# A two-layer hybrid trunk on one core: kept weight chunks of layer two's first query/key pair in slots of their own, two more slots for the token sums, the forget gate's tile in another slot

## The chip, the cores and the metric

The kernel runs on one core of one Trainium2 chip. The metric is device time in microseconds (us) of one execution. Before the change three runs took 1605.53, 1605.92 and 1603.42 us; the median is 1605.53. The trace is one profiled execution of the same program.

Engines are named as the profile names them: PE is TensorE's matmul, PEld its weight load, DVE is VectorE, ACT is ScalarE, POOL is GpSimd and SP is SyncE, which issues most of the DMAs. L246 is line 246 of the kernel.

## The reference

Two layers (DEPTH = 2) over 512 tokens of width 2048, in float32. Each layer normalises x, maps it through one input projection, and splits the result by columns into a gated linear attention group and a chunked attention group, each with a SiLU gate. Their outputs go through one output projection and are added to x:

```python
h = rmsnorm(x, g_pre)
z = h @ w_in
gq, gk, gv, gg, ga, aq, ak, av, ag = split_columns(z)
log_a = jax.nn.log_sigmoid((ga @ w_alpha + b_alpha).astype(jnp.float32)) / GLA_TAU
o_gla = gla_chunk_causal(...)            # chunk-wise state recurrence with the forget gate log_a
o_gla = rmsnorm(o_gla, ...) * jax.nn.silu(gg)
o_att = chunk_band_attention(...)        # softmax over the own chunk and the 8 before, with a relative bias
o_att = rmsnorm(o_att, ...) * jax.nn.silu(ag)
y = jnp.concatenate([o_gla, o_att], axis=-1) @ w_out
return x + rmsnorm(y, g_post)
```

## The kernel before

**Products.** The weights are cut into column blocks of 512 (the blocks of `AG1` and `AG2` have 264) and into chunks of 256 rows. Every float32 operand is split into a high part (a cast on ACT, line 236, written `wh` for weights) and a low part (a subtraction on DVE, line 246, `wl`), and a product takes three matmuls: high by high, low by high, high by low.

Two blocks that lie side by side make a pair. A pair is not multiplied in eight block products of the four quarters of tokens and features, but in seven, P1 to P7, each over four chunks (c = 0 to 3), as in Strassen's method in Winograd's form. On the token side this needs four sums, S1 to S4, per chunk; on the weight side sums are made while the pair runs. One weight chunk is kept through the whole pair: P1 loads it (`H`), P5 adds another chunk to it, P6 adds a third, P7 subtracts it from a fourth, P2 adds to it again, and P4 uses it last. So the four `H` tiles of a pair stay in use from its first product to its last. Other weight chunks (`raw`) and sums (`sa`) live in rings for one or two products.

A job is one product with one chunk. For each of the pair's jobs the stream loads (`load`), adds and casts (`high`), makes the low part (`low`), and then PE runs twelve matmuls (24 of half the width for the query/key pairs, which are computed feature by feature, line 430). Loads, casts and low parts are made three to five jobs ahead of PE (`ahead`).

**Layer two, in the order of the program.** The standard product of block `AG0` (line 353) and the pair `AV0, AV1` are interleaved, since the second half of the tokens comes late out of layer one. Then comes the narrow gate pair `AG1, AG2` (matmuls of 264 columns), then the first query/key pair `QK01, QK23`, then the second, `QK45, QK67`.

**Token sums.** `token_sums(1)` runs as a task beside the second half of `AG0` and the rest of the `AV0` pair. For each chunk c it makes S1, S3, S2 and S4 in this order: a subtraction or addition on DVE, the high part on ACT (line 108), the low part on DVE (line 109). Then POOL issues a DMA that writes the sum to DRAM (line 618), from where later pairs load it again. S1 and S2 also stay in slots of their own (`HOMES`: S1 in g9, g14, g15, g2, S2 in g12, g13, g8, g11) and are read there by P5 and P6 of the `AV0` and the gate pair. S3 and S4 only pass through staging slots, which are used in turn: g10, g16 and a tile of the `H` ring. A staging slot can be written again when its DMA to DRAM has landed.

**Rings and slots.** `H` is a ring of four tiles, `raw` of five, `sa` and `wh` of four, `wl` of three. The gate pair's four kept chunks take the four `H` tiles, and each comes free when the gate pair's P4 has cast it. `slot(tag)` is a fixed place of SBUF that takes a new tile when the last reader of the old one is through. g0 and g1 hold two operands (`A21`, chunks 2 and 3) of the standard product `AG0`, and later values of the attention group.

**What sets the order.** Each engine runs its instructions in the order in which they stand in the program. A scheduler sets that order when the program is built, from a timeline of its own; so a change of a tile's place also moves other instructions. SP issues DMAs in its own order; a DMA that has to wait for a free tile holds up those behind it.

**Forget gate.** `load_forget_gate(l)` (line 758) loads w_alpha into the tile `raw`, in slot g12, which is also the home of S2 of chunk 0; `forget_gate` uses it at the end of the gate pair.

Of the kernel before, what the change touches and what calls it, by code (L numbers as in the profile page):

```python
# [36 lines left out]
def hybrid_trunk(  # L37
# [113 lines left out]
    class Job:  # L151
# [23 lines left out]
        def load(self):  # L175
            k, c, p, b0, b1 = self.kind, self.c, self.pair, self.b0, self.b1
            end = b0 >= NB_IN and k != "std"
            if end:
                c = OC[c]
            top, bottom = (c + 4, c) if end else (c, c + 4)  # L180
            mid = end and b0 == W23[0] and self.l < L - 1
            if k == "std":
                self.raw = self.fetch(rtile("raw", bufs=5), b0, c)
            elif k == "P1":
                h = slot(f"g{4 + c}", [2, 512]) if self.parted else rtile("H")
                p["H", self.c] = self.fetch(h, b0, top)
                last_h[0] = last_load[0]
            elif k == "P5" and self.parted:
                h = p["H", c]
                src = w[self.l, b1 - (b1 > AG1), top].rearrange("p (k n) -> p k n", k=2)  # L190
                nc.gpsimd.dma_start(h, src, accum_op=ALU.add)
            elif k == "P5":
                p["r", self.c] = self.fetch(rtile("raw", bufs=5), b1, top)
            elif k == "P6":
                p["r", self.c] = p["b22", self.c] = self.fetch(rtile("raw", bufs=5), b1, bottom)
            elif k == "P7":
                p["r", self.c] = p.pop(("t", self.c), None) or self.fetch(rtile("raw", bufs=5), b0, top)
            elif k == "P2" or (k == "P4" and (end or self.parted)):
                p["r", self.c] = self.fetch(rtile("raw", bufs=5), b0, bottom)
            sums = (so_d if end else sa_d)[self.l]  # L200
            src = sums.get((LEFT.get(k), c))
            if self.l == L - 1:
                home = k in ("P5", "P6") and b0 in (AV0, AG1)
            else:
                home = k == "P5" and b0 == AV0
            if b0 == AG1 and k == "P5":
                p["a22", c] = slot(f"g{4 + c}", [2, 512], F32R)
                nc.sync.dma_start(flat(p["a22", c]), sums["A22", c])
            if b0 == AG1 and k == "P4":
                self.a = p["a22", c]  # L210
            elif src is not None and b0 != NB_IN and not home:
                until(lambda: k == "P4" or (id(sums), LEFT[k], c) in written)
                self.a = rtile("sa", (2, 512), F32R)
                with tc.issue_after(last_h[0]) if mid else nullcontext():
                    last_load[0] = nc.sync.dma_start(flat(self.a), src).ins
            if b0 == W23[0] and k == ("P6" if mid else "P5"):
                with tc.issue_after(last_h[0]):
                    p["t", self.c] = self.fetch(slot(f"a11{self.c}" if mid else SPARE[self.c], [2, 512]), b0, c + 4)
# [36 lines left out]
    for l in range(L):  # L255
        if l:
            pr = {}
            stream += [Job(l, "std", c, AG0) for c in CO]
            stream += [Job(l, k, c, *PAIRS[0], pr) for k, c in PROD_FRONT]
            stream += [Job(l, "std", c, AG0) for c in CO]  # L260
            stream += [Job(l, k, c, *PAIRS[0], pr) for k, c in PROD_REST]
            pr = {}
            stream += [Job(l, k, c, *GATE_PAIR, pr) for k, c in PROD_GATE]
        else:
            stream += [Job(l, "std", c, b) for b in (AG0, AG1, AG2) for c in CO]
        for b0, b1 in PAIRS[1:] if l else PAIRS:
            pr = {}
            stream += [Job(l, k, c, b0, b1, pr) for k, c in PROD]
        for b0, b1 in (W01, W23):
            pr = {}  # L270
            stream += [Job(l, k, c, b0, b1, pr) for k, c in (PROD_OUT if b0 == NB_IN else PROD_END)]
# [363 lines left out]
            yield  # L635

    def token_sums(l):
        tags, home = (("g10", "g16", "H"), HOMES) if l else (STAGE, HOME)
        return make_sums(sa_d[l], tags, lambda c: (full[0, c][:, 0, :], full[0, c][:, 1, :], full[1, c][:, 0, :], full[1, c][:, 1, :]), home)

    VT = ("g16", "g17", "g4", "g5", "g6", "g7", "g12", "g13")
# [114 lines left out]
    fg_weights = {}  # L756

    def load_forget_gate(l):
        raw = slot("g12", [2, 512])
        fac = slot("g13", [2, 512], F32R)  # L760
        nc.sync.dma_start(raw[0:98, 0, :], w_alpha[l])
        nc.gpsimd.memset(raw[96:98, 1, :], 1.0)
        wal, gaT = fac[0:98, 0, :], fac[0:98, 1, :]
        yield
        nc.scalar.copy(wal, raw[0:98, 0, :])
        nc.vector.tensor_tensor(
            out=wal[64:97, :], in0=raw[64:97, 0, :], in1=wal[64:97, :].bitcast(F32), op=ALU.subtract
        )
        fg_weights[l] = (raw, fac, wal, gaT)
        yield  # L770
# [815 lines left out]
```

## Time and profile before

| | |
|---|---|
| median of three runs | 1605.53 us (1603.42 to 1605.92) |
| the profiled execution | 1608.99 us, its span 1607.2 us |
| DMA in the span | 441.38 MB, mean 275 GB/s |
| mean granted clock of PE | 0.998 |
| gate pair (window 924.35 to 971.84) | 47.5 us, P1 to P4 of 264 columns |
| first query/key pair | from 971.84 us |

How to read the views: a row of the timeline gives the start in us from the span's start, the duration of the group, engine, line, operation, tiles written and read, shapes and count, and in brackets how long the engine stood idle before it and what ended that. A window row gives length, then busy time and count of PE, PEld, DVE, ACT and POOL, then the granted clock of PE, the mean busy share of the DMA engines, and GB/s.

### The profile page before, as it was taken

The numbers are of one execution on the slowest core, as the hardware profiler recorded it, in microseconds if no ns is written. First come the engines' busy times: TensorE is split into PE (matmuls) and PEld (weight loads), VectorE is DVE, ScalarE is ACT, GpSimd is POOL, SyncE is SP. The second block draws the span as 40 slices with busy tenths as digits, with TensorE's granted clock in tenths as the row PEclk, the third lists the DMA queues.
The fourth block names the chain that finished last, engine by engine and source line by source line (L and its number), as shares of the span: only waits on it lengthen the run. The fifth ranks groups of instructions, "written<-read, shape, count | busy, mean of one in ns | idle before, by whom it ended". The sixth has DMA issues, their size and how long they took to land.

```text
span 1607.2 us, 25131 instructions
## 1 busy us (share of the span) xinstructions
PE 1592.8 (99%) x9158; PEld 1376.8 (86%) x9158; DVE 1278.0 (80%) x1697; ACT 920.5 (57%) x1535; POOL 134.2 (8%) x206
## 2 busy tenths in 40 slices
PE   9999999999999999999999999999999999999998
PEld 7988999998888777888887899999988887788886
DVE  5978768678677877998988877775876878689887
ACT  7554445657454556664786455456575545465654
POOL 0220000000000001100122000000000100101001
PEclk9999999999999999999999999999999999999999
DMA  9798686685868769689889987857858686686887
GB/s 351 232 407 304 220 295 216 228 307 170 275 220 281 270 210 319 217 309 389 306 259 364 361 282 280 308 186 260 301 202 298 202 305 242 227 299 241 331 303 205
DMA packets 137228, 441.38 MB, mean 275 GB/s; under 512 B 14885, under 2 KB 27429, under 8 KB 137073
## 3 DMA queue, kind: packets, MB, share of 16 engines
q1 hardware_dynamic: 119952, 377.86, 67.0%
q0 software_dynamic: 16864, 61.63, 10.9%
q8 instruction: 72, 1.18, 0.3%
q14 instruction: 52, 0.42, 0.1%
q10 hardware_dynamic: 288, 0.30, 0.1%
HBM read 380.20 MB, written 61.62 MB: 275 GB/s over the span
## 4 chain that ended last, share of the span: by engine, by line
PE 88%; issue 4%; DMA 3%; DVE 3%; ACT 1%; POOL 1%; POOLq 0%; SPq 0%; ACTq 0%; DVEq 0%
PE mm L440 51%; PE mm L430 20%; PE mm L353 5%; PE ax L440 3%; PE ax L1007 2%; DMA H<-in_w_dram 2%; PE ax L1193 1%; PE ax L990 1%; PE ax L1165 1%; DVE wl L246 1%; PE ax L970 1%; PE ax L969 1%; PE ax L968 1%; DMA S<-g 1%; ACT wh L236 0%
## 5 line engine op out<-in xcount | busy, mean ns | idle before, releaser
L440 PE MATMUL mm<-wh,sa 128*128 128x512 f32 (+1 forms) x1600 | 510.1, 390 | 1.2 <-DMA sa<-S 0.6
L236 ACT CAST wh<-H 128x1024 fp32r<-128x1024 f32 (+1 forms) x256 | 261.5, 1025 | 207.8 <-PE mm L440 80.3
L246 DVE TENSOR_TENSOR wl<-H,wh 128x1024 fp32r<-128x1024 f32 (+1 forms) x256 | 303.4, 1188 | 92.8 <-PE mm L440 28.1
L440 PEld LDWEIGHTS mm<-wh,sa 128*128 128x128 f32 x1600 | 297.6, 188 | 70.6 <-issue 8.1
L236 ACT CAST wh<-raw 128x1024 fp32r<-128x1024 f32 (+2 forms) x237 | 236.3, 1001 | 194.1 <-PE mm L440 71.7
L246 DVE TENSOR_TENSOR wl<-raw,wh 128x1024 fp32r<-128x1024 f32 (+2 forms) x237 | 272.9, 1154 | 59.2 <-PE mm L440 24.6
L440 PE MATMUL mm<-wl,sa 128*128 128x512 f32 (+1 forms) x800 | 309.2, 387 | 0.0
L430 PE MATMUL mm<-sa,wh 128*128 128x256 f32 x1280 | 238.1, 285 | 0.2 <-ACT wh L236 0.2
L440 PE MATMUL mm<-wh,a 128*128 128x512 f32 (+1 forms) x672 | 218.2, 389 | 0.0
L430 PEld LDWEIGHTS mm<-sa,wh 128*128 128x128 f32 x1280 | 200.6, 192 | 0.9 <-ACT wh L236 0.4
L430 PE MATMUL mm<-sa,wl 128*128 128x256 f32 x640 | 180.8, 283 | 0.0
L440 PEld LDWEIGHTS mm<-wl,sa 128*128 128x128 f32 x800 | 150.3, 188 | 28.8 <-DVE wl L246 0.4
L230 DVE TENSOR_TENSOR H<-H,raw 128x1024 f32<-128x1024 f32 (+1 forms) x144 | 170.2, 1187 | 1.9 <-DMA raw<-in_w_dram 1.2
L440 PEld LDWEIGHTS mm<-wh,a 128*128 128x128 f32 x672 | 124.8, 188 | 25.1
L440 PE MATMUL mm<-wl,a 128*128 128x512 f32 (+1 forms) x336 | 130.2, 388 | 0.0
L430 PEld LDWEIGHTS mm<-sa,wl 128*128 128x128 f32 x640 | 122.2, 191 | 0.2 <-DVE wl L246 0.2
L440 PE MATMUL mm<-wh,g 128*128 128x512 f32 (+1 forms) x416 | 120.3, 367 | 0.2
L484 POOL TENSOR_TENSOR sm<-sm,mhalf 128x2 f32<-128x2 f32 (+2 forms) x40 | 50.1, 1252 | 684.3 <-DVE sm L1017 376.7
L232 DVE TENSOR_TENSOR raw<-H,raw 128x1024 f32<-128x1024 f32 (+1 forms) x56 | 66.4, 1186 | 42.1 <-DMA raw<-in_w_dram 39.8
L390 ACT COPY ev<-mm 128x512 f32<-128x512 f32 (+1 forms) x112 | 64.1, 572 | 59.2 <-PE mm L440 44.1
L430 PE MATMUL mm<-a,wh 128*128 128x256 f32 x512 | 95.7, 287 | 1.4 <-ACT wh L236 1.4
L252 DVE TENSOR_TENSOR H<-H,raw 128x1024 f32<-128x1024 f32 (+1 forms) x48 | 56.6, 1180 | 43.0 <-DMA raw<-in_w_dram 40.7
(273 smaller groups left out, 2411.9 us busy)
## 6 DMA issues: line engine op xcount, KB each, us to landing
raw<-in_w_dram SPq DMA_DIRECT2D x287, 512.0 KB, 5.1
sa<-S SPq DMA_DIRECT2D x188, 512.0 KB, 4.4
H<-in_w_dram SPq DMA_DIRECT2D x60, 512.0 KB, 5.1
sa<-A SPq DMA_DIRECT2D x48, 512.0 KB, 5.6
sa<-oS SPq DMA_DIRECT2D x32, 512.0 KB, 5.4
S<-g POOLq DMA_DIRECT2D x30, 512.0 KB, 7.9
raw<-in_w_ag_dram SPq DMA_DIRECT2D x32, 264.0 KB, 4.2
oS<-g POOLq DMA_DIRECT2D x16, 512.0 KB, 4.7
```

Of the source, the lines that this page charges most:

```text
L230: nc.vector.tensor_tensor(out=h, in0=h, in1=r, op=ALU.add)
L232: nc.vector.tensor_tensor(out=r, in0=h, in1=r, op=ALU.subtract)
L236: last_cast[0] = nc.scalar.copy(self.wh[:, z, :], src[:, z, :]).ins
L246: last_low[0] = nc.vector.tensor_tensor(out=self.wl[:, z, :], in0=self.src[:, z, :], in1=self.wh[:, z, :].bitcast(F32), op=ALU.subtract).ins
L252: nc.vector.tensor_tensor(out=h, in0=h, in1=self.src, op=ALU.add)
L353: nc.tensor.matmul(pss[o], a(part, kk, o) if callable(a) else a[:, part, t], rhs[:, kk, :], start=(i == 0 and kk == 0 and m == 0), stop=(i ...
L390: last_copy[0] = nc.scalar.copy(e, src[t]).ins
L430: nc.tensor.matmul(dst, lhs[:, kk, f], a[:, part, tok], start=(fresh and kk == 0 and m == 0 and ft % 2 == 0), stop=(c == 3 and kk == 1 and ...
L440: last_mm[0] = nc.tensor.matmul(out_ps[t], a[:, part, tok], rhs[:, kk, :], start=(fresh and kk == 0 and m == 0), stop=(c == 3 and kk == 1 ...
L484: nc.gpsimd.tensor_tensor(out=out_r, in0=v, in1=mhalf[:, : v.shape[-1]], op=ALU.pow)
L968: nc.tensor.matmul(ps[:, :n], self.qh[:, t], self.kh[:, :n], start=True, stop=False)
L1007: nc.tensor.matmul(o, self.pt[i][:, j * P : (j + 1) * P], av[hd // 4, j // 2][:, j % 2, (hd % 4) * P : (hd % 4 + 1) * P], start=(j == 0), ...
```

## The change

Three things change, all in layer two.

First, P1 of the first query/key pair loads nothing any more: its four kept chunks are loaded by P3 of the gate pair, into the slots g14, g15, g2 and g12, the homes of S1 of chunks 1 to 3 and of S2 of chunk 0. The dictionary `qk` hands them from one pair to the other. The gate pair's `H` tiles, which used to go to these chunks, go to the kept chunks of the second query/key pair. Second, the staging slots of the token sums are five: g10, g16, `H`, g0, g1. Third, the forget gate's tile is in g10 in layer two.

```diff
             if k == "std":
                 self.raw = self.fetch(rtile("raw", bufs=5), b0, c)
+            elif k == "P1" and ("H", self.c) in p:
+                pass
             elif k == "P1":
                 h = slot(f"g{4 + c}", [2, 512]) if self.parted else rtile("H")
                 p["H", self.c] = self.fetch(h, b0, top)
...
+            if b0 == AG1 and k == "P3":
+                p["next"]["H", c] = self.fetch(slot(("g14", "g15", "g2", "g12")[c], [2, 512]), PAIRS[1][0], c)
...
-            pr = {}
+            qk = {}
+            pr = {"next": qk}
             stream += [Job(l, k, c, *GATE_PAIR, pr) for k, c in PROD_GATE]
...
         for b0, b1 in PAIRS[1:] if l else PAIRS:
-            pr = {}
+            pr = qk if l and b0 == QK01 else {}
             stream += [Job(l, k, c, b0, b1, pr) for k, c in PROD]
...
-        tags, home = (("g10", "g16", "H"), HOMES) if l else (STAGE, HOME)
+        tags, home = (("g10", "g16", "H", "g0", "g1"), HOMES) if l else (STAGE, HOME)
...
-        raw = slot("g12", [2, 512])
+        raw = slot("g10" if l else "g12", [2, 512])
```

The order of the instructions moves with it, from the token sums of layer two to the end of the first query/key pair; outside that stretch it is the same. The lines of the changed kernel stand a few numbers later (246 becomes 250). A name such as g16_1717_8817 is a tile in slot g16 and its serial number.

**ACT and DVE during the token sums** (between the last standard products and the rest of the `AV0` pair). L108 is the high part of a sum, wh the cast of a weight chunk: wh_1720 for P5 of chunk 1, wh_1723 for chunk 2, wh_1729 for chunk 3, wh_1736 for P6 of chunk 0. The serial number after the slot tells the sum: 1713 is S4 of chunk 1, 1716 and 1717 are S1 and S3 of chunk 2, 1725 is S3 of chunk 3. ACT before:

```order
L108 CAST g10_1713_8790<-H_1573_8105 128x512
L108 CAST g16_1717_8817<-g2_1645_8451 128x512
L236 CAST wh_1720_8840<-g5_1668_8546 128x1024
L108 CAST g15_1716_8812<-g2_1645_8451 128x512
L236 CAST wh_1723_8862<-g6_1671_8564 128x1024
L782 ACTIVATE t2_1726_8881<-mm_1693_8681 128x512
L236 CAST wh_1729_8897<-g7_1674_8582 128x1024
```

ACT now:

```order
L108 CAST g0_1713_8790<-H_1573_8105 128x512
L240 CAST wh_1720_8840<-g5_1668_8546 128x1024
L108 CAST g15_1716_8812<-g2_1645_8451 128x512
L108 CAST g1_1717_8817<-g2_1645_8451 128x512
L240 CAST wh_1723_8862<-g6_1671_8564 128x1024
L108 CAST g16_1725_8871<-g3_1653_8485 128x512
L787 ACTIVATE t2_1726_8881<-mm_1693_8681 128x512
L240 CAST wh_1729_8897<-g7_1674_8582 128x1024
```

S3 of chunk 2 stands two places later on ACT, behind P5's cast and S1 of chunk 2, and S3 of chunk 3 has come up. On DVE, which makes the low parts of the same sums (L109) and weights (L250) and the additions to the kept chunks (L234 for P5 and P6, L236 for P7), the twelve rows from S4 of chunk 1 on are now:

```order
L109 TENSOR_TENSOR g0_1713_8790<-H_1573_8105,g0_1713_8790 128x512
L234 TENSOR_TENSOR g4_1660_8521<-g4_1660_8521,raw_1730_8899 128x1024
L109 TENSOR_TENSOR g15_1716_8812<-g2_1645_8451,g15_1716_8812 128x512
L250 TENSOR_TENSOR wl_1722_8860<-g5_1668_8546,wh_1720_8840 128x1024
L109 TENSOR_TENSOR g1_1717_8817<-g2_1645_8451,g1_1717_8817 128x512
L635 TENSOR_TENSOR g2_1645_8451<-g2_1645_8451,H_1581_8144 128x512
L109 TENSOR_TENSOR g16_1725_8871<-g3_1653_8485,g16_1725_8871 128x512
L234 TENSOR_TENSOR g5_1668_8546<-g5_1668_8546,raw_1737_8928 128x1024
L250 TENSOR_TENSOR wl_1728_8895<-g6_1671_8564,wh_1723_8862 128x1024
L236 TENSOR_TENSOR raw_1754_9025<-g4_1660_8521,raw_1754_9025 128x1024
L638 TENSOR_TENSOR H_1581_8144<-H_1581_8144,g2_1645_8451 128x512
L109 TENSOR_TENSOR g8_1718_8828<-g2_1645_8451,g8_1718_8828 128x512
```

Three rows of 1024 columns follow up to the low part for P6 of chunk 0: the low part for P5 of chunk 3, an addition, and that low part itself. Before, the second of these rows was the low part of S3 of chunk 2 (in g16), ahead of the addition to g4.

**SP and PE in the gate pair.** SP issues the raw chunks of AG1 and AG2 (raw, from in_w_ag) and the sums (sa, from S3). SP before, from P3's last raw chunk on:

```order
L164 DMA raw_1853_9525<-in_w_ag_dram 128x528
L164 DMA raw_1859_9562<-in_w_ag_dram 128x528
L164 DMA raw_1863_9583<-in_w_ag_dram 128x528
L761 DMA g12_1934_9963<-in_w_alpha_dram 98x512
L164 DMA raw_1867_9604<-in_w_ag_dram 128x528
L215 DMA sa_1860_9564<-S310_110 128x1024
L164 DMA raw_1871_9625<-in_w_ag_dram 128x528
```

SP now:

```order
L164 DMA raw_1856_9531<-in_w_ag_dram 128x528
L172 DMA g14_1834_9425<-in_w_dram 128x1024
L164 DMA raw_1863_9570<-in_w_ag_dram 128x528
L172 DMA g15_1841_9464<-in_w_dram 128x1024
L164 DMA raw_1867_9591<-in_w_ag_dram 128x528
L172 DMA g2_1852_9511<-in_w_dram 128x1024
L172 DMA g12_1859_9550<-in_w_dram 128x1024
L164 DMA raw_1871_9612<-in_w_ag_dram 128x528
L219 DMA sa_1864_9572<-S310_110 128x1024
L164 DMA raw_1875_9633<-in_w_ag_dram 128x528
```

The four kept chunks have come in between the raw chunks, and w_alpha has gone from there; it is issued some 34 places earlier. At the head of the gate pair PE had, ahead of P4 of chunk 2 of the `AV0` pair (mm_1664, mm_1665, twelve matmuls of which the first two are shown), two matmuls of the gate's first job (mm_1816, mm_1817):

```order
L440 MATMUL mm_1816_9328<-wh_1800_9259,a110_1563_8075 128x264
L440 MATMUL mm_1817_9329<-wh_1800_9259,a110_1563_8075 128x264
L440 MATMUL mm_1664_8528<-wh_1789_9210,sa_1787_9193 128x512
L440 MATMUL mm_1664_8528<-wl_1795_9235,sa_1787_9193 128x512
L440 MATMUL mm_1664_8528<-wh_1789_9210,sa_1787_9193 128x512
```

and now has all twelve of them there (the first six shown):

```order
L445 MATMUL mm_1816_9328<-wh_1800_9259,a110_1563_8075 128x264
L445 MATMUL mm_1817_9329<-wh_1800_9259,a110_1563_8075 128x264
L445 MATMUL mm_1816_9328<-wl_1803_9277,a110_1563_8075 128x264
L445 MATMUL mm_1816_9328<-wh_1800_9259,a110_1563_8075 128x264
L445 MATMUL mm_1817_9329<-wl_1803_9277,a110_1563_8075 128x264
L445 MATMUL mm_1817_9329<-wh_1800_9259,a110_1563_8075 128x264
```

The matmuls that read the low part wl_1803 have moved up, ahead of P4 of chunk 2.

**SP at the start of the first query/key pair.** The raw chunks are those of P5 (the first two) and P6, sa is S1, and the H tiles are kept chunks. Before:

```order
L172 DMA raw_1912_9862<-in_w_dram 128x1024
L172 DMA raw_1921_9909<-in_w_dram 128x1024
L215 DMA sa_1939_9999<-S112_104 128x1024
L172 DMA H_1906_9826<-in_w_dram 128x1024
L215 DMA sa_1944_10041<-S113_105 128x1024
L172 DMA raw_1938_9997<-in_w_dram 128x1024
L172 DMA H_1909_9844<-in_w_dram 128x1024
L172 DMA raw_1943_10039<-in_w_dram 128x1024
L172 DMA H_1916_9883<-in_w_dram 128x1024
```

Now:

```order
L172 DMA raw_1914_9866<-in_w_dram 128x1024
L219 DMA sa_1923_9913<-S111_103 128x1024
L172 DMA raw_1922_9911<-in_w_dram 128x1024
L219 DMA sa_1939_9999<-S112_104 128x1024
L172 DMA H_2043_10768<-in_w_dram 128x1024
L172 DMA raw_1938_9997<-in_w_dram 128x1024
L219 DMA sa_1944_10041<-S113_105 128x1024
L172 DMA H_2051_10813<-in_w_dram 128x1024
L172 DMA raw_1943_10039<-in_w_dram 128x1024
L172 DMA H_2072_10914<-in_w_dram 128x1024
```

The H tiles in these places were the first query/key pair's kept chunks; now they are the second's (their serial numbers are higher), which used to be issued about 40 places later.

On ACT the casts of the first two kept chunks now stand ahead of the gate pair's last evictions and of the table load; before, only the first did. On POOL the memset of the forget gate's tile stands before the last two sums' writes; before, it stood behind them.

## The prediction

> **What bounds the kernel now.** I read the page first: busy times, then the chain that ended last.
>
> ```profile
> PE 1592.8 (99%) x9158; PEld 1376.8 (86%) x9158; DVE 1278.0 (80%) x1697; ACT 920.5 (57%) x1535; POOL 134.2 (8%) x206
> PE 88%; issue 4%; DMA 3%; DVE 3%; ACT 1%; POOL 1%; POOLq 0%; SPq 0%; ACTq 0%; DVEq 0%
> ```
>
> TensorE (PE) is the bound, and the change adds and removes no matmul. So it can only win back time in which PE waits, or runs below its pace. A pipelined PE looks busy even then; pauses have to be read from matmul starts against an undisturbed pace. These windows give the pace: 50 us hold 419 matmuls of the query/key form, two of them still running from before, so 0.12 us each; 21.56 us hold 95 new ones with 512 columns, so 0.227 us each.
>
> ```profile
> 990.00:1040.00 50.00, 50.00 (x419) 50.00 (x419) 35.80 (x35) 25.00 (x29) 0.00 (x0) 1.00 0.80 276
> 852.06:873.62 21.56, 21.56 (x96) 17.83 (x95) 17.46 (x23) 12.52 (x17) 4.36 (x9) 1.00 1.01 386
> ```
>
> **Place 1, the start of the first query/key pair.** PE's timeline, the count of that line's matmuls (L430), and the granted clock (after the busy times) around the pause:
>
> ```profile
> 971.84 0.63 PE L430 MATMUL mm<-a,wh 128*128 128x256 f32 x4
> 976.48 0.74 PE L430 MATMUL mm<-a,wh 128*128 128x256 f32 x4 [1.40 <-ACT wh L236]
> 977.43 1.17 PE L430 MATMUL mm<-sa,wh 128*128 128x256 f32 x4 [0.21 <-ACT wh L236]
> 981.19 0.40 PE L430 MATMUL mm<-a,wh 128*128 128x256 f32 x2
> 971.84:981.30 9.46, 7.85 (x47) 7.29 (x48) 0.82 1.00 392
> 974.80:980.74 5.94, 4.33 (x22) 3.92 (x21) 4.28 (x4) 4.76 (x7) 0.94 (x2) 0.73 0.98 395
> ```
>
> From the first of the 47 starts (971.84) to the last (981.19) are 46 steps: 46 x 0.12 = 5.52 us at pace, 9.35 us in fact. **3.83 us are lost.** The clock row splits them: (1 - 0.73) x 5.94 = 1.6 us at a lowered clock, about 2.2 us of pauses. What ended last before them, from the chain and from ACT's timeline:
>
> ```profile
> 961.06 8.90 DMA H<-in_w_dram
> 957.51 1.63 SPq L172 DMA_DIRECT2D raw<-in_w_dram  x2
> 970.06 1.05 ACT L236 CAST wh<-H 128x1024 fp32r<-128x1024 f32 x1 [1.74 <-DMA H<-in_w_dram]
> 974.09 1.28 ACT L62 ACT_TABLE_LOAD   x1
> 975.38 1.99 ACT L236 CAST wh<-H 128x1024 fp32r<-128x1024 f32 x2
> ```
>
> The SP row is P5's first two raw loads. The pair's first kept chunk is issued at 961.06, lands at 970, and only then can ACT cast it. ACT is in order: behind that late cast came the gate evictions and a table load, so the second chunk was cast at 975.38.
>
> **Place 2, the token sums.**
>
> ```profile
> 881.78 0.61 PE L440 MATMUL mm<-wh,g 128*128 128x512 f32 x2
> 883.47 0.73 PE L440 MATMUL ax<-wh,g 128*128 128x512 f32 x2 [1.07 <-ACT g L108]
> 887.63 0.84 PE L440 MATMUL ax<-wh,g 128*128 128x512 f32 x3
> 882.20:887.50 5.30, 4.12 (x17) 2.94 (x17) 5.30 (x7) 2.29 (x4) 2.14 (x4) 1.00 0.94 303
> 871.89 0.62 ACT L108 CAST g<-g 128x512 fp32r<-128x512 f32 x1 [3.66 <-DMA S<-g]
> 872.54 0.69 DVE L109 TENSOR_TENSOR g<-g,g 128x512 fp32r<-128x512 f32 x1 [2.56 <-ACT g L108]
> 880.80 0.62 ACT L108 CAST H<-H 128x512 fp32r<-128x512 f32 x1 [2.48 <-DVE H L633]
> 882.80 0.61 ACT L108 CAST g<-g 128x512 fp32r<-128x512 f32 x1
> ```
>
> Between 881.78 and 887.63 start 18 matmuls (the window's 17 and the one before them): 18 x 0.227 = 4.08 us at pace, 5.85 in fact, **1.77 us lost**, at full clock. PE waits for S1 of chunk 3, cast at 882.80. That is late because S3 of chunk 2 waited till 871.89 for slot g16, which was still being written out; DVE stood for 2.56 us behind it and was busy without a break afterwards.
>
> **The change, part by part.** *Kept chunks.* The four loads of 512 KB now have slots g14, g15, g2, g12, free once P5 of chunks 1, 2, 3 and P6 of chunk 0 are through in the gate pair. SP issues them between the gate's raw loads, near 936 to 944 us. DMA's share there (the figure before GB/s):
>
> ```profile
> 936.00:940.00 4.00, 4.00 (x35) 4.00 (x35) 3.73 (x6) 1.92 (x4) 0.00 (x0) 1.00 0.42 129
> 940.00:944.00 4.00, 4.00 (x35) 4.00 (x34) 3.45 (x6) 3.10 (x7) 0.52 (x1) 1.00 0.29 73
> 944.00:948.00 4.00, 4.00 (x35) 4.00 (x34) 2.23 (x4) 2.02 (x4) 0.00 (x0) 1.00 0.79 244
> ```
>
> At the 392 GB/s of the saturated window above, 2.1 MB take 5.3 us. Free are 4 x (0.58 + 0.71 + 0.21) = 6.0 us. They fit, just, and land some 25 us before use. The vacated places on SP, from 961 us on, do not stay empty: the next pair's H loads move up into the ring, so P5's raw chunks land as late as before. They have time: P1 of chunks 0 and 1 needs no load and keeps PE busy for 48 x 0.12 = 5.8 us, until 977.6; P5's first raw loads are issued from 957.51 on. ACT now casts both P1 chunks ahead of the evictions and the table load. I take the whole 3.83 us as gone; the other end is 0. Late next would be P5 of chunk 1, wanted four chunks on, at 971.84 + 4 x 2.88 = 983.4. ACT comes to its cast after the table load, which ended at 975.4, and some five casts of 1.05, near 981; DVE's low part takes 1.2 more: about 1 us of room, an estimate.
>
> One rule speaks against part of this. By the Trainium skill's page "TensorE: Matmul & The Clock Gate" (section "HAM oscillation — how this bites in real kernels") only PE pauses over about 3.4 us bring the lower clock back. Here it does not agree with the trace, where pauses of 1.4 and 0.2 us stand beside the 0.73 above. By the rule, the 1.6 us would have another cause and stay, and the sum below would be 3.45.
>
> *Two more slots.* S4 of chunk 1 goes to g0, S3 of chunk 2 to g1. A wait is exchanged, not removed: g1 holds an operand of the standard product until PE has read it, and ACT's queue is behind it.
>
> ```profile
> 870.68 0.39 PE L353 MATMUL mm<-wh,g 128*128 128x512 f32 x1
> 869.30 0.69 DVE L109 TENSOR_TENSOR g<-H,g 128x512 fp32r<-128x512 f32 x1
> 874.29 0.69 DVE L109 TENSOR_TENSOR g<-g,g 128x512 fp32r<-128x512 f32 x1
> 874.89 1.22 DVE L246 TENSOR_TENSOR wl<-g,wh 128x1024 fp32r<-128x1024 f32 x1
> 876.02 0.68 DVE L630 TENSOR_TENSOR g<-g,H 128x512 f32<-128x512 f32 x1
> ```
>
> That read ends at 871.07, only 0.8 us before 871.89. But in the new order a cast of P5's weights and S1 of chunk 2 stand ahead of the waiting one, so DVE has work meanwhile. From 869.9 it has eight operations of 1024 columns (1.14 us apart) and six of 512 (0.60 apart) up to the low part for P6 of chunk 0: 9.1 + 3.6 = 12.7, done at 882.6. PE asks for it at 881.78 + 6 x 0.227 = 883.1. ACT has S1 of chunk 3 by about 880 to 881.6, before the 882.24 at which PE wants it. So I take 1.77 us; the lower end is 0, since the room on DVE is 0.5 us.
>
> *Head of the gate pair.* Here the new order of PE costs. The low part of the gate's first chunk is ready late:
>
> ```profile
> 924.35 0.40 PE L440 MATMUL mm<-wh,a 128*128 128x264 f32 x2
> 924.38 0.71 DVE L246 TENSOR_TENSOR wl<-H,wh 128x528 fp32r<-128x528 f32 x1
> ```
>
> Before, twelve matmuls of P4 stood between the first two and those that need it; now these follow directly, at 924.59, while it ends at 925.09. About 0.55 us lost (everything shifts alike, since DVE's work there follows PE's evictions); ends 0 and 0.7.
>
> *Gate pair's end.* A small stall there hangs on a raw chunk for a DVE addition:
>
> ```profile
> 961.67 0.28 PE L440 MATMUL mm<-wh,g 128*128 128x264 f32 x1
> 962.33 0.39 PE L440 MATMUL ax<-wl,a 128*128 128x264 f32 x1 [0.37 <-DVE wl L246]
> 959.70 0.71 DVE L252 TENSOR_TENSOR H<-H,raw 128x528 f32<-128x528 f32 x1 [1.37 <-DMA raw<-in_w_ag_dram]
> ```
>
> 0.66 - 0.12 = 0.54 us. The raw loads move up a place on SP, the transfers before them grow. I take no change, between -0.54 and +0.5.
>
> *Forget gate tile.* w_alpha goes to g10, far earlier on SP; the wait for g12 (P6 of chunk 0) passes to the last kept chunk. POOL's memset now waits for S4 of chunk 2 to be written out, with the last two sums' writes behind it. Cost nothing: they are read long after.
>
> ```profile
> 895.05 0.53 POOL L618 DMA_DIRECT2D S<-g  x1 [0.21 <-issue]
> ```
>
> **The sum.** 3.83 + 1.77 - 0.55 = 5.05 us. The profiled execution took 1608.99 us (span 1607.2): 1603.9. Against the median of the runs, 1605.53, which is 3.46 shorter: **1600.5 us**.
>
> **Rivals.** *(a) The token sums stay late*: g1's wait or DVE's 0.5 us of room is misjudged. For it speaks the thin room, against it DVE's idle 2.56 us. Then 3.83 - 0.55 = 3.28: 1602.3. *(b) The lowered clock is not caused by these pauses* and returns anyway; the stall at 882, which kept clock 1.00 with a similar pause, speaks for it. 1.6 us stay: 1602.1. That rule of the Trainium skill would have it so. *(c) The change misses its aim*: the pair's start is held by something else (P5's raw chunks, ACT's order). Gain 1.77 - 0.55: 1604.3. *(d) Slower: the 2.1 MB do not fit* into 936 to 948 us. S3's operands and the last raw chunks of the gate pair queue behind them, and DMA is full from 964 on, so the 5.3 us are not made up: PE loses them before the query/key pair, with one lowered clock of 1.6: -5.05 + 5.3 + 1.6 = +1.85, 1607.4. It decides when more than about 3.7 us of transfers are left over: S3's first operand was issued at 944.97 and lands in 4.4, at 949.4; P7's first matmul, the second of the PE row, reads it at 953.1.
>
> ```profile
> 944.97 0.33 SPq L215 DMA_DIRECT2D sa<-S  x1
> sa<-S SPq DMA_DIRECT2D x188, 512.0 KB, 4.4
> 953.02 0.41 PE L440 MATMUL mm<-wh,sa 128*128 128x264 f32 x2
> ```
>
> **How the numbers follow.** Forecast 0.58, (a) 0.17, (b) 0.08, (c) 0.12, (d) 0.05. The low end: all three stalls gone and no loss at the head is 6.14 us, 1599.4, and 1 us for the spread of the runs (1603.42 to 1605.92): 1598.4. The high end takes in (c): 1604.6; (d) is left out. A measurement of this kernel tells 0.2%, 3.2 us, from no change. So faster means under 1602.3: the forecast, half of (a), most of (b), 0.71. Slower, over 1608.7, is the tail of (d), 0.04. The same: 0.25.
>
> **What would show it.** Right: in the changed profile the first query/key matmuls start 0.12 us apart over two chunks at clock 1.00; the kept chunks' issues stand at 934 to 943 us; no PE wait near 882; one of about 0.5 near 923 to 925. Wrong: a wait of PE on a low part at P6 of chunk 0 (a); a clock under 1.00 with no pause (b); ACT waiting for a DMA of raw at the pair's start (c); DVE or PE waiting for raw or sa between 945 and 965 (d).

## The result, and the profile after

Eighteen runs of each kernel: before 1606.76 us median (1603.42 to 1610.6), after 1603.04 us (1601.56 to 1607.24). The ratio is 0.9979, 95% interval 0.9971 to 0.9987: 3.4 us faster, between 2.1 and 4.7. A second measurement of the same change (below, e4) gave 0.9976 (0.9966 to 0.9986), 3.9 us. The prediction had 5.05 us and 1600.5, its range 1598.4 to 1604.6. So the time lies in the range, but the forecast gain lies above the first interval and inside the second (2.2 to 5.5).

The profiled execution after took 1601.56 us, its span 1599.5. That is 7.4 us less than the profiled execution before, twice what the medians say. How that comes about takes up most of what follows.

The head of the page and of the chain that ended last, after:

```profile
PE 1589.6 (99%) x9158; PEld 1375.0 (86%) x9158; DVE 1279.6 (80%) x1697; ACT 921.1 (58%) x1535; POOL 135.5 (8%) x206
PE 93%; DVE 3%; DMA 1%; ACT 1%; issue 1%; SPq 0%; POOLq 0%; DVEq 0%; ACTq 0%
```

PE has the same 9158 matmuls and is still the bound. Windows after, first one over the first 46 steps of the query/key pair, then the three over the stretch where the early loads were expected, then the token sums' stretch (columns as in the table's note above):

```profile
969.01:974.53 5.52, 5.52 (x49) 5.52 (x48) 5.52 (x9) 4.41 (x8) 0.69 (x3) 1.00 1.03 409
936.00:940.00 4.00, 4.00 (x35) 4.00 (x35) 2.97 (x5) 3.18 (x8) 0.00 (x0) 1.00 0.80 230
940.00:944.00 4.00, 4.00 (x35) 4.00 (x34) 2.52 (x5) 1.42 (x4) 0.00 (x0) 1.00 0.88 263
944.00:948.00 4.00, 4.00 (x35) 4.00 (x35) 3.91 (x7) 2.84 (x5) 0.00 (x0) 1.00 1.01 353
868.00:890.00 22.00, 22.00 (x98) 18.21 (x97) 21.64 (x25) 14.31 (x20) 5.77 (x12) 1.00 1.02 391
```

46 steps of 0.12 us are 5.52 us: the window holds those starts and three matmuls more (still running from before, or at its edge), at clock 1.00. Before, the same steps took 9.35. The DMA share between 936 and 948 rose from 0.42, 0.29 and 0.79; the differences sum to 4 x (0.38 + 0.59 + 0.22) = 4.8 us of the 5.3 that the new loads were priced at. PE is busy through all 22 us of the token sums, where it had been busy for 20.82 before:

```profile
868.00:890.00 22.00, 20.82 (x91) 16.61 (x90) 19.44 (x23) 12.22 (x18) 5.36 (x10) 1.00 1.00 378
```

PE's timeline after, the start of the query/key pair and the head of the gate pair; then ACT's row for S3 of chunk 2, now in slot g1, and SP's rows for the early loads:

```profile
969.01 0.64 PE L435 MATMUL mm<-a,wh 128*128 128x256 f32 x4
922.61 0.39 PE L445 MATMUL mm<-wl,a 128*128 128x264 f32 x1 [0.47 <-DVE wl L250]
```

```profile
870.25 0.62 ACT L108 CAST g<-g 128x512 fp32r<-128x512 f32 x1 [1.14 <-PE mm L358]
```

```profile
933.96 0.33 SPq L172 DMA_DIRECT2D g<-in_w_dram  x1
937.10 0.33 SPq L172 DMA_DIRECT2D g<-in_w_dram  x1
939.75 1.90 SPq L172 DMA_DIRECT2D g<-in_w_dram  x2
```

All four places are as forecast: the pair's start at pace, the new stall at the gate pair's head (matmul start to start 0.76 us, 0.64 over pace), the wait for g1 put on PE's read instead of a write-out, the loads between 934 and 942 us.

### The profile page after: what moved, and what is told of

It is laid out like the page before. It is cut to its first block, busy times and chain, and to the rows that moved or that the text cites. A ratio compares the mean times of both kernels' runs of the same rounds, so it can differ in the third digit from the quotient of the medians.

```text
span 1599.5 us, 25116 instructions
## 1 busy us (share of the span) xinstructions
PE 1589.6 (99%) x9158; PEld 1375.0 (86%) x9158; DVE 1279.6 (80%) x1697; ACT 921.1 (58%) x1535; POOL 135.5 (8%) x206
## 3 DMA queue, kind: packets, MB, share of 16 engines
q8 instruction: 72, 1.18, 0.3%
## 4 chain that ended last, share of the span: by engine, by line
PE 93%; DVE 3%; DMA 1%; ACT 1%; issue 1%; SPq 0%; POOLq 0%; DVEq 0%; ACTq 0%
PE mm L445 54%; PE mm L435 19%; PE mm L358 6%; PE ax L445 4%; PE ax L1012 2%; PE ax L1198 1%; DVE wl L250 1%; PE ax L995 1%; PE ax L1170 1%; DMA raw<-in_w_dram 1%; PE ax L975 1%; PE ax L974 1%; PE ax L973 1%; PE ax L1037 0%; PE ax L1290 0%
## 5 line engine op out<-in xcount | busy, mean ns | idle before, releaser
L240 ACT CAST wh<-H 128x1024 fp32r<-128x1024 f32 (+1 forms) x240 | 244.9, 1023 | 194.7 <-PE mm L445 81.2
L250 DVE TENSOR_TENSOR wl<-H,wh 128x1024 fp32r<-128x1024 f32 (+1 forms) x240 | 284.4, 1187 | 86.8 <-PE mm L445 31.3
L250 DVE TENSOR_TENSOR wl<-raw,wh 128x1024 fp32r<-128x1024 f32 (+2 forms) x237 | 273.2, 1156 | 60.2 <-PE mm L445 29.2
L234 DVE TENSOR_TENSOR H<-H,raw 128x1024 f32<-128x1024 f32 (+1 forms) x136 | 161.0, 1188 | 1.4 <-DMA raw<-in_w_dram 0.7
L236 DVE TENSOR_TENSOR raw<-H,raw 128x1024 f32<-128x1024 f32 (+1 forms) x52 | 61.6, 1184 | 34.8 <-DMA raw<-in_w_dram 34.6
L445 PEld LDWEIGHTS mm<-wh,g 128*128 128x128 f32 x416 | 75.3, 188 | 13.4 <-ACT ev L395 0.6
```

Source lines behind the costliest of these rows:

```text
L234: nc.vector.tensor_tensor(out=h, in0=h, in1=r, op=ALU.add)
L236: nc.vector.tensor_tensor(out=r, in0=h, in1=r, op=ALU.subtract)
L240: last_cast[0] = nc.scalar.copy(self.wh[:, z, :], src[:, z, :]).ins
L250: last_low[0] = nc.vector.tensor_tensor(out=self.wl[:, z, :], in0=self.src[:, z, :], in1=self.wh[:, z, :].bitcast(F32), op=ALU.subtract).ins
L445: last_mm[0] = nc.tensor.matmul(out_ps[t], a[:, part, tok], rhs[:, kk, :], start=(fresh and kk == 0 and m == 0), stop=(c == 3 and kk == 1 ...
```

## The experiments

The losses below are worked out from the starts of all matmuls between the 4,801st (844.16 us before, 843.31 after) and the 6,001st (1034.47 and 1028.20; outside this stretch the order did not change): the time from start to start less the number of steps at pace (0.227 us for 512 columns, 0.12 for 256 and 264, 0.06 for 128). Undisturbed steps of 264 columns take 0.121 us on the mean, so some 0.3 us of each profile's gate pair is this rounding; it cancels in differences.

| run | edit | median us (runs) | ratio, 95% interval |
|---|---|---|---|
| e1 | kernel before again | 1606.11 (12) | 0.9993 (0.9982 to 1.0004) |
| e2 | token sums' two slots alone | 1607.75 (12) | 0.9999 (0.9989 to 1.0009) |
| e3 | kept chunks' early loads alone | 1604.91 (12) | 0.9984 (0.9972 to 0.9996) |
| e4 | the change again | 1603.35 (12) | 0.9976 (0.9966 to 0.9986) |
| e5 | first kept chunk loaded twice | 1621.48 (1) | |
| e6 | one token slot less | 1610.26 (1) | |
| e7 | one early chunk | 1605.11 (11) | 0.9983 (0.9973 to 0.9992) |
| e8 | the five slots in another order | 1605.95 (11) | 0.9995 (0.9986 to 1.0004) |
| e9 | one early chunk, five slots | 1604.64 (12) | 0.9980 (0.9969 to 0.9991) |
| e10 to e12 | kernel before, three profiles | 1609.39, 1607.16, 1607.85 | |

The kernel before ran beside them with medians of 1606.97 to 1607.45 us.

### e1, e10, e11, e12: the kernel before, four more profiles

No edit. The question is whether the stalls of the one profile from which the prediction was sized are those of every execution.

> The kernel before, unchanged, for a second profile of it. Open is why the profiled executions lie 7.4 us apart and the medians only 3.7. Theory A (every execution of the kernel before has the three stalls at the sizes of its first profile): again 1.8 us lost at 882, 0.5 at 961.7, and 3.8 at 972 to 981 with a granted clock near 0.73 there; time within 0.1% of before. Theory B (the lowered clock at 975 is not in every execution): the two pauses of 1.4 and 0.2 us stand there again, but the clock is 1.00 in that window and only about 2.2 us are lost; the ratio is 1.000 all the same.

> A third profile of the kernel before. Theory B (what the first profile shows at 882 and at 975 was a draw from a spread): between 0.3 and 1.8 us lost at 868 to 890, 1.5 to 2.6 us of pauses and casts late at 972 to 982, and a lowered clock only if the pauses fall together in one stretch of some 3.4 us, as in the first profile. Theory A: 1.8 and 3.8 as in the first.

> A fourth profile of the kernel before, with the same expectations as the third: theory B gives losses between those of the first two profiles, theory A the first profile's.

> A fifth profile of the kernel before, with the same expectations as the third. Over the five, theory B has the mean of what the change removes between 844 and 1034 us near the 3.4 to 3.9 us of the ratios; theory A has it at 5 or more.

ACT's wait for g16's write-out, in e1, e10, e11 and e12 in turn (before: 3.66):

```profile
870.68 0.62 ACT L108 CAST g<-g 128x512 fp32r<-128x512 f32 x1 [2.28 <-DMA S<-g]
```

```profile
872.48 0.62 ACT L108 CAST g<-g 128x512 fp32r<-128x512 f32 x1 [3.25 <-DMA S<-g]
```

```profile
871.07 0.62 ACT L108 CAST g<-g 128x512 fp32r<-128x512 f32 x1 [2.54 <-DMA S<-g]
```

```profile
872.16 0.62 ACT L108 CAST g<-g 128x512 fp32r<-128x512 f32 x1 [2.19 <-DMA S<-g]
```

PE's losses behind it were 0.38, 1.37, 0.64 and 0.31 us, and 1.77 in the first profile: in each of the five the wait less 1.9 us. So the wait was read rightly, and 1.9 us of it are covered by what DVE and PE have in hand; but the landing of the write-out differs by 1.5 us between executions, and the first profile held the longest of the five.

PE's pause before the second chunk of the query/key pair, in e1, e10, e11 and e12 in turn (before: 1.40; a pause of 0.21 follows in all):

```profile
975.16 0.74 PE L430 MATMUL mm<-a,wh 128*128 128x256 f32 x4 [0.83 <-ACT wh L236]
```

```profile
977.73 0.74 PE L430 MATMUL mm<-a,wh 128*128 128x256 f32 x4 [1.41 <-ACT wh L236]
```

```profile
976.12 0.74 PE L430 MATMUL mm<-a,wh 128*128 128x256 f32 x4 [1.39 <-ACT wh L236]
```

```profile
977.10 0.74 PE L430 MATMUL mm<-a,wh 128*128 128x256 f32 x4 [1.42 <-ACT wh L236]
```

The pause is there in all five. The clock behind it isn't. Windows of 3.4 us over pause and what follows, in the kernel before, e10 and e12:

```profile
974.10:977.50 3.40, 1.79 (x14) 1.38 (x12) 1.12 (x2) 3.27 (x3) 1.61 (x3) 1.00 1.03 414
977.50:980.90 3.40, 3.40 (x16) 3.40 (x17) 3.40 (x4) 2.36 (x4) 0.00 (x0) 0.50 0.92 371
```

```profile
976.34:979.74 3.40, 1.80 (x13) 1.60 (x14) 2.03 (x2) 3.30 (x5) 0.66 (x2) 1.00 1.02 406
979.74:983.14 3.40, 3.40 (x19) 3.40 (x18) 3.40 (x4) 2.12 (x4) 0.00 (x0) 0.50 0.75 261
```

```profile
974.10:977.50 3.40, 1.98 (x17) 1.78 (x16) 1.12 (x2) 3.36 (x6) 2.17 (x4) 1.00 1.02 410
975.70:979.10 3.40, 1.78 (x12) 1.58 (x13) 2.02 (x2) 2.82 (x4) 0.66 (x2) 1.00 1.02 408
977.50:980.90 3.40, 3.19 (x27) 2.98 (x26) 3.40 (x4) 2.82 (x5) 0.00 (x0) 1.00 0.87 346
```

Two of the five (the first and e10) ran at half clock for 3.4 us; e11 and e12, with the same pause, and e1 did not. At half clock the matmuls of this form start 0.213 us apart (16 in 3.4 us) instead of 0.12, so the drop costs 16 x 0.093 = 1.5 us where it comes, where the prediction took 1.6. All losses together:

| losses, us | before | e1 | e10 | e11 | e12 | mean | after | e4 | gain, means | forecast |
|---|---|---|---|---|---|---|---|---|---|---|
| token sums | 1.77 | 0.38 | 1.37 | 0.64 | 0.31 | 0.89 | 0.00 | 0.00 | 0.89 | 1.77 |
| to the gate pair's head | 0.13 | 0.83 | 0.16 | 0.25 | 0.05 | 0.28 | 0.80 | 0.82 | -0.53 | -0.55 |
| rest of the gate pair | 1.37 | 1.34 | 1.18 | 1.46 | 0.76 | 1.22 | 0.47 | 0.48 | 0.75 | 0 |
| query/key start, 100 steps | 3.83 | 1.55 | 4.60 | 2.57 | 3.34 | 3.18 | 0.00 | 0.00 | 3.18 | 3.83 |
| from there on | 0.00 | 0.00 | 0.52 | 0.00 | 0.61 | 0.23 | 0.40 | 0.31 | -0.13 | 0 |
| sum | 7.10 | 4.10 | 7.83 | 4.92 | 5.07 | 5.80 | 1.67 | 1.61 | 4.16 | 5.05 |

Theory B: the five span 4.1 to 7.8 us of losses, and what the change removes on their mean, 4.2 us, lies within both intervals of the timed runs. Its bounds were too narrow, though: e10 lost more than the first profile, and e12 3.34 us at the start without a drop of the clock. Theory A, that each execution has the first profile's sizes, does not hold. The rest of the 7.4 us between the two profiled executions lies outside the stretch that was changed, 0.85 us of it already before 844.

### e4: the change again

> The changed kernel, unchanged, for a second profile beside these. Theory A: no loss over 0.3 us between 860 and 1015 us but the one at the head of the gate pair (0.6), ratio 0.9968. Theory B: the same profile, ratio 0.9979, the sum of the two single parts within 1 us.

Its losses stand in the table: within 0.06 us of the first profile after in sum. In these two profiles, what the change leaves did not vary; in the five before, what it removed did.

### e2 and e3: one part alone

e2 is the kernel before with the slots only:

```diff
-        tags, home = (("g10", "g16", "H"), HOMES) if l else (STAGE, HOME)
+        tags, home = (("g10", "g16", "H", "g0", "g1"), HOMES) if l else (STAGE, HOME)
```

> Only the two more slots for the token sums. Theory A: the stall at 882 goes (-1.8 us), the one at the head of the gate pair comes (+0.6), the start of the query/key pair stays as it was: -1.2 us, ratio 0.9993. Rival (the token sums are late for another reason than slot g16's write-out): a stall of 1 us or more stays near 882 and the kernel is not faster, ratio 1.000 or 1.0004 with the head's stall.

e3 is the change with that line as before.

> Only the kept chunks' loads in slots g14, g15, g2, g12, with the forget gate's tile in g10; the token sums keep three slots. Theory A: 1.8 us at 882 stay, no stall at the head of the gate pair, the 3.8 us at the query/key pair's start and perhaps the 0.5 us at 961.7 go: -3.8 to -4.4 us, ratio 0.9975. Theory B (lowered clock only in some executions): -2.2 to -2.8 us, ratio 0.9984. Rival (P5's raw chunks hold the start): under 1 us, ratio above 0.9994.

e3 removes the start's whole loss, and is 0.9984, 2.6 us faster (0.6 to 4.5); theory B's number. e2 has no loss at the token sums, 0.81 at the gate pair's head as expected, and still gains nothing. PE's timeline, then SP's, in e2:

```profile
954.49 0.39 PE L440 MATMUL mm<-wl,sa 128*128 128x264 f32 x1 [0.35 <-DVE wl L246]
959.83 0.51 PE L440 MATMUL mm<-wh,sa 128*128 128x264 f32 x2 [1.10 <-DMA sa<-S]
```

```profile
951.65 3.13 SPq L164 DMA_DIRECT2D raw<-in_w_ag_dram  x2
954.88 0.38 SPq L215 DMA_DIRECT2D sa<-S  x1
```

With the token sums' slots the scheduler also puts a raw load of the gate pair ahead of the last operand's load (`sa`) on SP. The raw load waits for a free tile, the operand behind it is issued at 954.88, and PE waits for it until 959.83. The rest of the gate pair loses 2.46 us, where the five profiles of the kernel before have 1.22. What PE loses there it waits less at the query/key pair's start (0.69 us), since it comes there later, at 972.97. That the start's loss shrinks when PE is late, because the kept chunk's landing does not move with PE, is argued from this and not shown by itself. Over the whole stretch e2's profile even loses less than the mean of the five, 4.35 us against 5.80, while the timed runs have a difference of 0.2 us, between 1.8 faster and 1.4 slower. So the late operand by itself does not explain why no gain is seen, and that stays open.

So the gains don't simply add up: -0.2 and -2.6 us of the parts against -3.4 and -3.9 of the whole, though the intervals leave room for a sum.

### e5: the first kept chunk one load later

```diff
             elif k == "P1":
                 h = slot(f"g{4 + c}", [2, 512]) if self.parted else rtile("H")
+                if self.l and b0 == QK01 and c == 0:
+                    self.fetch(h, b0, top)
                 p["H", self.c] = self.fetch(h, b0, top)
```

> The kernel before, with the query/key pair's first kept chunk loaded twice into its tile, so that it is complete one load (4 to 9 us) later. Theory (the landing of the kept chunk holds the pair's start): PE loses 4 to 8 us more around 972 to 985 than the 2.5 to 3.8 of the two profiles of the kernel before, time near 1610 to 1614. Rival (something else holds it): under 1 us more. On the clock: if a pause of PE lowers it, this one of several us does so more surely than the 1.4 us of the first profile, and the granted clock falls below 0.9 behind it; if the clock stays at 1.00 here, the 0.73 of the first profile was not caused by the pause alone.

PE's and ACT's timelines, and windows from PE's stop on:

```profile
982.65 1.22 PE L432 MATMUL mm<-a,wh 128*128 128x256 f32 x4 [10.79 <-ACT wh L238]
```

```profile
981.55 1.99 ACT L238 CAST wh<-H 128x1024 fp32r<-128x1024 f32 x2 [7.97 <-DMA H<-in_w_dram]
```

```profile
971.50:974.50 3.00, 0.36 (x3) 0.15 (x2) 0.00 (x0) 2.03 (x3) 1.96 (x4) 0.98 1.02 418
974.50:982.50 8.00, 0.00 (x0) 0.00 (x0) 0.00 (x0) 0.94 (x1) 0.00 (x0) 0.50 0.70 285
982.50:988.00 5.50, 5.31 (x23) 5.01 (x24) 5.34 (x5) 2.83 (x4) 0.00 (x0) 0.50 0.11 35
988.00:992.00 4.00, 4.00 (x35) 4.00 (x35) 4.00 (x7) 2.99 (x5) 0.00 (x0) 0.99 0.66 218
```

The time is 1621.48 us, above the 1610 to 1614 expected. The start loses 13.6 us instead of 1.6 to 4.6: the chain from the chunk's landing over ACT's cast to PE is the one that holds the pair's start. The size was missed: 9 to 12 us more, not 4 to 8, since the second load lands only at 981.5, where the first profile had the chunk at 970.06. The clock fell at 974.39 in the trace's clock record, after 2.5 us of pause (PE stopped at 982.65 - 10.79 = 971.86), and stayed at half until 988.0, 5.4 us after PE had gone on.

### e6: one staging slot less

```diff
-        tags, home = (("g10", "g16", "H"), HOMES) if l else (STAGE, HOME)
+        tags, home = (("g10", "g16"), HOMES) if l else (STAGE, HOME)
```

> The kernel before with one staging slot less for the token sums (g10 and g16, without the H tile). Theory (they wait for a slot that is still being written out): the waits of ACT for a write-out grow and PE loses more than 1.8 us between 868 and 890. Rival (the write-out's landing mattered only in the first profile, and two slots are enough): under 0.8 us lost there. The start of the query/key pair is that of the kernel before, and so gives one more sample of it: 2 to 4 us lost, less by what PE has lost shortly before.

```profile
867.36 1.14 ACT L108 CAST g<-g 128x512 fp32r<-128x512 f32 x2 [5.46 <-DMA S<-g]
```

The row is ACT's. The wait for a write-out grows to 5.46 us and PE's loss at the token sums to 3.51: the rival, that two slots are enough, falls. Its query/key start (1.34 us of pause, clock 1.00) lost 2.05, with 7.1 us lost ahead of it in the stretch.

### e7: one early chunk

The change's loads for chunk 0 alone; token sums and forget gate as before.

```diff
-            if b0 == AG1 and k == "P3":
+            if b0 == AG1 and k == "P3" and c == 0:
```

> Only the first of the four kept chunks is loaded early, into g14; chunks 1 to 3 come through the H ring, token sums and forget gate as before. Theory 1 (the first late cast holds the rest of ACT's queue, and the next chunk moves up to its place on SP): the start runs at pace over two chunks, the gain is that of all four (ratio 0.9984). Theory 2 (each chunk is late by itself): a pause of 1 us or more stays at the second or third chunk, ratio 0.9992 or above.

Window over the first 46 steps, then ACT's timeline around them:

```profile
972.06:977.58 5.52, 5.52 (x49) 5.52 (x48) 5.52 (x6) 4.48 (x9) 1.11 (x3) 1.00 1.03 414
```

```profile
967.92 1.05 ACT L240 CAST wh<-g 128x1024 fp32r<-128x1024 f32 x1 [0.63 <-PE ax L445]
970.41 1.05 ACT L240 CAST wh<-H 128x1024 fp32r<-128x1024 f32 x1 [0.91 <-DMA H<-in_w_dram]
977.23 1.28 ACT L62 ACT_TABLE_LOAD   x1
```

Theory 1: the pair starts at pace, and the ratio is that of e3. Chunk 1 still lands late, and ACT waits 0.91 us for it; but with chunk 0 out of the way its cast comes at 970.41, ahead of the table load and the evictions that used to stand before it, and PE wants it only one chunk later. The other three early loads are not needed for the start.

### e8 and e9: attempts to do better

e8 has the same five slots in another order, meant to keep PE's old order at the gate pair's head:

```diff
-        tags, home = (("g10", "g16", "H", "g0", "g1"), HOMES) if l else (STAGE, HOME)
+        tags, home = (("g0", "g10", "g16", "H", "g1"), HOMES) if l else (STAGE, HOME)
```

> The changed kernel with the five staging slots in another order (g0, g10, g16, H, g1). The order of PE at the head of the gate pair is then that of the kernel before. Theory: the stall of 0.64 us near 922 goes and nothing near 882 comes back: 0.6 us faster than the change, ratio 0.9972 to before where the change has 0.9976 to 0.9979. Rival (the stall moves on, or other sums wait): no faster than the change, with a new loss of 0.3 us or more between 840 and 960.

```profile
881.66 0.97 PE L445 MATMUL ax<-wh,g 128*128 128x512 f32 x3 [0.34 <-DVE g L109]
923.38 0.51 PE L445 MATMUL mm<-wh,a 128*128 128x264 f32 x2 [0.89 <-ACT wh L240]
```

The rival: PE's rows show the stall moved. The token sums lose 1.67 us again, this time for DVE's low part of a sum, and the gate pair's head 1.23, for ACT's cast instead of DVE's low part. The old order was not kept: the gate's first two matmuls are the 5,135th and 5,136th of the program here, and the 5,147th and 5,148th in the kernel before, so PE asks for that cast twelve matmuls (2.7 us) earlier. The ratio of 0.9995 is above the change's 0.9976 and 0.9979, though the intervals just touch. What the old order itself would give is not shown.

e9 is the change with e7's line.

> The changed kernel, but only the first of the four kept chunks loaded early. Theory (one early chunk frees ACT's queue, and the token slots add what they add beside the four): as the change, ratio 0.9976 to 0.9979. Rival (with the new order of the token sums, chunks 1 to 3 come late out of the H ring): a pause of 0.5 us or more at 972 to 985 and a ratio of 0.9985 or above.

```profile
954.48 0.39 PE L445 MATMUL mm<-wl,sa 128*128 128x264 f32 x1 [0.65 <-DVE wl L250]
961.88 0.39 PE L445 MATMUL mm<-wl,g 128*128 128x264 f32 x1 [0.98 <-DVE wl L250]
```

```profile
960.49 0.71 DVE L256 TENSOR_TENSOR H<-H,raw 128x528 f32<-128x528 f32 x1 [2.45 <-DMA raw<-in_w_ag_dram]
```

The time cannot be told from the change's (0.9980), and the start runs at pace, so the rival falls. But its profile has the gate pair's rest at 3.28 us of losses, where the change has 0.47: PE's two rows wait for DVE, and DVE's row for a raw chunk that lands late; from 100 steps on it loses 1.41 more. Its highest run, 1608.26, is the profiled one. No version measured beats the change.

## Why the prediction was right, and where its sizes were off

**The bound, and the two places.** Right. Nothing but PE's pauses could be won, and the two named ones are gone, by the chains that were named: e5 for the kept chunk's landing, e6 and the five waits less 1.9 us for g16's write-out.

**Place 1, 3.83 us.** Right in kind, 3.18 on the mean of five profiles. Mis-sized is the 1.6 us of lowered clock, which stands in two profiles of five and is 1.5 there, 0.6 on the mean. Rival (b), that the drop is not a plain consequence of the pauses, was right in that much: the same 1.4 and 0.2 us bring it in the first profile and e10, and not in e11 and e12; the last section shows where the difference lies. Since the change removes the pauses too, the drop went with them, and (b)'s price of 1.6 us was not paid.

**Place 2, 1.77 us.** Right in kind, 0.89 on the mean. The term was read from the longest of five waits. DVE's room, put at 0.5 us, was enough: it is busy for 21.64 of the 22 us in the window after, and PE loses nothing. Rival (a) falls. The exchanged wait stands in ACT's row after at 870.25; 0.85 us, by which that execution is ahead there, put it at 871.10 in the frame of before, where the prediction had 871.07. No timed run shows a gain of these slots by themselves: e2 is at 0.9999, and the change (0.9976 and 0.9979) cannot be told from e3 without them (0.9984).

**Gate pair's head, -0.55.** 0.64 us for the pause itself, -0.53 in the table's means. The prediction's own rows gave 925.09 - 924.59 = 0.50.

**Gate pair's end, taken as 0, bounded at -0.54.** The stall went whole, and the rest of the gate pair gained 0.75 us on the means, more than the bound; no step there is more than 0.1 us over pace after the change. The raw chunks of DVE's additions land in time after the change (they carried a wait of 1.37 us for a DMA before):

```profile
954.95 1.32 DVE L256 TENSOR_TENSOR H<-H,raw 128x528 f32<-128x528 f32 x2
957.95 0.70 DVE L256 TENSOR_TENSOR H<-H,raw 128x528 f32<-128x528 f32 x1
```

The step had seen that the raw loads move up a place on SP and weighed the fuller queues against it. e3, with the same early loads, loses 0.53 us in that part of the pair, so the four early loads and the order that comes with them on SP seem to bring it; e7, with one of them, still loses 1.07, within the 0.76 to 1.46 of the kernel before.

**The loads' room and rival (d).** They fit, with 4.8 us of the 6.0 used, and nothing waits for raw or sa between 945 and 965. **P5's chunks** were not late, and rival (c) falls. **The forget gate's tile**, taken as nothing, was not tested alone: e3 has it moved and e7 not, and their ratios are 0.9984 and 0.9983.

**The sum.** 5.05 us forecast; 4.16 on the profiles' means, 3.4 and 3.9 by the timed runs. By the gain alone rivals (a), 3.28, and (b), 3.45, fit better; it is the profile, with no loss at the token sums and clock 1.00, that decides against them. What is off is a step that the text did not state: that one profiled execution has the stalls of a typical one. Of the 2.5 us between 1600.5 and 1603.04, 1.2 is the median before, which three runs put at 1605.53 and eighteen at 1606.76; 1.3 is the gain's size. 1603.04 is also above the 1602.3 under which the prediction, with 0.71, spoke of faster. Part of the nearness is luck: on the means the three terms of the sum come to 0.89 + 3.18 - 0.53 = 3.54, and the gate pair's end, put at nothing, brings 0.75. In the first profile itself the same places were worth 5.43 us (7.10 - 1.67), and the three terms to 1.77 + 3.83 - 0.67 = 4.93, so the working of the sum was sound for that execution.

## What to carry to other kernels

Here the stalls that ended with the landing of a DMA had another length in each execution: take several profiles before a term of a few tenths of a per cent is priced, above all where the runs before spread more than the gain. When an in-order engine opens a stage with a cast that waits for a load, one early load for the first chunk can be enough, since the rest of its queue was only standing behind it. Where a scheduler sets the order, a part tested alone is another order too: in the profile of the slots alone, PE waited for a load that had slipped behind another on SP.

## What the runs showed of the hardware that was not expected

The lowered clock came in whole stretches of 3.4 us at 0.50, 977.5 to 980.9 in the first profile and 979.74 to 983.14 in e10, and they began 1.0 and 2.0 us after the end of the long pause (976.48 and 977.73). In the 3.4 us ahead of them PE was busy for 1.79 and 1.80 us. In e12, too, 3.4 us can be laid over the pause with PE busy for 1.78 us (975.70 to 979.10), and the clock stayed at 1.00 behind them. In e5 a pause of 10.79 us brought it down after 2.5 us, for 13.65 us, four times 3.41. This looks like a clock that is set for 3.41 us at a time by what PE did in the stretch before, with stretches that don't start with the pause.

The traces' clock records bear this out: in each of them the changes lie whole steps of 3.413 us apart. In the first profile the record begins at 4.72 us; the clock falls 285 steps later, at 977.52, returns at 980.94, and falls again 183 steps after that, at 1605.58, when the matmuls are over. In the other traces that last fall gives the steps near the pause. In e11 and e12, and in e6, with pauses of much the same length, the stretches that hold them are these (e11, e12 twice, e6):

```profile
973.03:976.44 3.41, 2.02 (x17) 1.81 (x16) 1.14 (x2) 3.38 (x6) 2.18 (x4) 1.00 1.03 411
972.98:976.39 3.41, 2.65 (x20) 2.44 (x20) 1.82 (x4) 2.99 (x6) 2.19 (x4) 1.00 1.02 414
976.39:979.80 3.41, 2.48 (x18) 2.28 (x19) 2.72 (x3) 2.85 (x4) 0.00 (x0) 1.00 1.02 406
977.59:981.01 3.42, 1.91 (x14) 1.50 (x13) 1.14 (x2) 3.38 (x4) 1.67 (x4) 1.00 1.02 410
```

PE was busy for 1.80 us of the stretch ahead of the fall in the first profile and e10, and for more in these: in e12 the long pause is split between two stretches, in e11 the short one falls into the next. The fourteen traces hold 6,546 such stretches at full clock: one with 1.80 us of PE or less is always followed by half clock, and one with 1.89 us or more (the lowest is 4.72 to 8.14 in the first profile) never is. In the token sums of the first profile, the stretch with the least work (881.95 to 885.36) has 2.23 us, which answers the prediction's doubt about that stall. So in these traces the fall follows from how the pauses lie on the steps; no run moved the steps on purpose.

The Trainium skill, page "TensorE: Matmul & The Clock Gate", section "What's actually happening", says that the half clock follows an idle window of about 3.4 us, and that the window runs freely and does not restart with the kernel. The length and the chance of phase agree with these traces. That the window has to be idle does not: PE was busy for 1.80 of the 3.41 us. By the rule on pauses as the prediction read it, that only pauses over 3.4 us count, the drop would have stayed in the changed kernel; neither profile of it has one, nor do those of e3, e7, e8 and e9, which start at pace too.
